# Value products of two dilated attention patterns: tokens in natural order, the permutation done by a store to and loads from DRAM

## The chip, the cores and the metric

The kernel runs on one core of a Trainium2 chip. A core has a matrix engine (TensorE, PE in the profile; its weight loads are shown apart, as PEld), a vector engine (DVE), a scalar engine (ACT), GpSimd (POOL) and SyncE (SP), which in this kernel issues every DMA. The metric is the device time of one execution in microseconds (us); less is better. Three runs of the kernel before gave 3298.71, 3296.22 and 3298.6 us, median 3298.6.

## The reference

The reference is a trunk of two layers over 1024 tokens with 1024 channels. Each layer has a mixer with four groups of heads that read the same normalised input, and a gated dense part. The change touches group D, dilated windowed attention with four heads and three patterns:

```python
D_PATTERNS = ((128, 1), (512, 4), (2048, 16))     # (window, dilation)
def to_strided(t, d):                             # tokens 0, d, 2d, ... become neighbours
    b, s, h, dh = t.shape
    return jnp.swapaxes(t.reshape(b, s // d, d, h, dh), 1, 2).reshape(b * d, s // d, h, dh)
...
o = jnp.einsum('nbhgqj,nbjhd->nbqhgd', p, vw.astype(jnp.float32)) / den
```

A pattern has its own queries, keys and values, 256 columns of the projection each. Within a residue modulo the dilation, attention is banded; the three patterns of a head meet under one softmax. What counts here is that the values of a dilated pattern are wanted ordered by (residue, index): first all tokens of residue 0, then of residue 1, and so on.

## The kernel before, in words

All products are made of three matmuls: each operand is split into a high and a low part (`hh`, `hl` for the input; `wh`, `wl` for weights), and high x high, high x low and low x high are added up in PSUM. `self.hh[k]` and `self.hl[k]`, k from 0 to 7, hold 128 channels each of the input, channels on partitions and the 1024 tokens along the free axis.

Group D runs pattern after pattern (p = 0, 1, 2): first `values(l, p)`, then for each pair of heads keys (`heads_k`), queries (`heads_q`) and scores (`scores_d`). Only when all three patterns have scores does `attend_d` multiply them with the values, through `weigh` (L628).

`values` makes values with tokens on partitions. For each of 8 token tiles it runs 8 x 3 matmuls (L587 to L589), so 192 for a pattern: the stationary operand, loaded into PE ahead of each matmul, is 128 tokens of `hh` or `hl`, and the moving operand is 256 columns of weights (288 for p = 0). The function `tokens` chooses the 128 tokens: for p = 0 neighbours, for p = 1 every fourth (residues of 4) and for p = 2 every eighth (residues of 8), so that the products come out in (residue, index) order. ACT copies each token tile from PSUM (pool `pj`, two buffers) to the tile `v` of the pattern (`put_v`, L554), beside a column of ones per head, which POOL sets once (L541).

A scheduler fixes the order of the instructions of each engine before the run; each engine works its list in order, and SP issues its DMAs in order. In layer 0 the list has work of other parts between group D's: `modulations` sums 48 pieces of a weight matrix of 256 KB each (`room<-in_w_mod`, L357 on SP; L360 and L362 on DVE; six buffers at a time; L402 to L425 fold each of three sums), and `rotary` makes tables: L329 on DVE, a sine on ACT (L331), L333 and L335 on DVE, eight transposes on PE (L340), copies on DVE (L342) and two stores `csd<-tn` on SP (L343). Layer 1 has neither within group D. Weights come from DRAM as `raw` (L116) and are split by ACT (L110) and POOL (L111). A tile of relative biases for scores comes by a DMA as well (`bias<-brep`, L601). `heads_k` and `heads_q` leave their PSUM by ACT (L507, L524) and DVE (L508, L526).

Of the kernel before, what the change touches and what calls it, by code (L numbers as in the profile page):

```python
# [48 lines left out]
DILATION = (1, 4, 8)  # L49

# [13 lines left out]
HALVES = (slice(0, 512), slice(512, 1024))  # L64

# [4 lines left out]
def _columns(name, i):  # L70
    c = np.arange(TILES_IN[name][i], TILES_IN[name][i] + 128)
    if name == "aq":
        # heads i and 2 + i: the key heads 0 and 1
        c = np.concatenate([np.arange(64 * i, 64 * i + 64), np.arange(64 * i + 128, 64 * i + 192)])
    return c
# [17 lines left out]
class Trunk:  # L93
# [14 lines left out]
    def split(self, hi, lo, src, eng=None):  # L108
        """hi + lo = src, both in the multiplier's format."""
        self.nc.scalar.activation(hi, src, AF.Copy)  # L110
        (eng or self.nc.gpsimd).tensor_sub(lo, src, hi.bitcast(F32))  # L111
# [10 lines left out]
    def gather(self, src, q, op, view=lambda x: x):  # L122
        """Reduces over the partitions; column f*32+j ends at [j, f] (rows 0..31)."""
# [16 lines left out]
    def spread(self, dst, r, f):  # L140
        """dst[p, f*32+j] = r[p//32*32+j, f]."""
        n = dst.shape[0]
        self.nc.vector.transpose(dst.rearrange("p (f i) -> p f i", i=32),
                                 r.unsqueeze(2).broadcast_to([n, f, 32]))

    def rstd(self, tiles, n, temp, adders=None):
        """Every row: rsqrt(mean over the tiles' channels of their squares + eps). The adders take turns in adding up
        the tiles."""
# [31 lines left out]
        # 3/8 of a guess at the root, a cubic step and a quadratic one  # L180
# [13 lines left out]
    def temps(self, pool=None, tag="", x=None, more=False):  # L194
        """Scratch tiles of 512 columns, from the pool or from the common ones."""
# [45 lines left out]
    def open_shared(self, name):  # L241
        """Room for the same tiles, which serves the latent attention first."""
# [18 lines left out]
    def tables(self):  # L261
        """Relative-bias rows."""
# [19 lines left out]
    def rotary(self):  # L282
        """The rotary tables."""
# [61 lines left out]
    def mod_sum(self, l, j, room=None):  # L345
        """Columns 1024*j.. of silu(c) @ w_mod[l], summed to 128 rows."""
# [19 lines left out]
    def mod_both(self, l, j, c, mr, mc):  # L366
        """As mod_sum for half c of the columns; the tensor engine takes the last of them, to one partition."""
# [18 lines left out]
    def mod_end(self, part):  # L386
        """mod[l] columns 1024*j .. with channels on partitions, b_mod added."""
# [8 lines left out]
    def mod_fold(self, part, t):  # L396
        """As mod_end, on the vector engine."""
# [15 lines left out]
    def mod_put(self, l, j, at, n, m):  # L413
# [3 lines left out]
        # scales and gates meet the norms' weights  # L417
# [15 lines left out]
    def modulated(self, src, l, g, j, hs, temp, adders=None, rs=None, ks=range(KT)):  # L433
        """hh, hl = split of rms_norm(src) * gain + shift, some of the tokens."""
# [14 lines left out]
    def residual(self, y, l, g, hs, xsrc, dst, temp, adders=None, rs=None):  # L449
        """y <- x + gain * rms_norm(y), also to dst."""  # L450
# [14 lines left out]
    def mm3(self, ps, wh, wl, xh, xl, first, last):  # L465
        """ps += w.T @ x with both split."""
# [5 lines left out]
    def product(self, ps, wh, wl, hs):  # L472
        """ps = w.T @ h for some of the tokens, the weights' low parts last."""
# [9 lines left out]
    def project(self, l, name, i, halves=(0, 1)):  # L483
        """A 128-channel tile of h @ w_in, yields (half, psum)."""
# [8 lines left out]
    def perm(self, ap, r):  # L493
        """View of natural token order on an axis that is kept as (residue, index)."""
# [18 lines left out]
    def heads_q(self, l, name, i, r=1):  # L513
        """High parts of each head on both halves of the partitions; low parts beside zeros."""
# [14 lines left out]
    def tokens(self, ap, tt, r):  # L529
        """128 columns of a [128, 1024] tile: token tile tt of the (residue, index) order."""  # L530
        if r == 1:
            return ap[:, 128 * tt:128 * tt + 128]
        n = 8 // r
        return ap.rearrange("p (l r) -> p r l", r=r)[:, tt // n, 128 * (tt % n):128 * (tt % n) + 128]

    def new_v(self, tag, heads, pool=None):
        """Room for the values, a column of ones after each head's, 32 columns after the last. Returns views of a
        token tile and head with 32 columns after the values, and of some token tiles' values."""
        v = (pool or self.vp).tile([128, 2112], F32, name="v", tag=tag)
        n = 520 * heads  # L540
        self.nc.gpsimd.memset(v[:, 0:n].rearrange("p (t c) -> p t c", c=65)[:, :, 64:65], 1.0)  # L541
# [8 lines left out]

        return taken, put
# [4 lines left out]
    def values_a(self, l):  # L556
        """Values of two heads, by way of channels on partitions, by halves of the tokens."""
# [12 lines left out]
    def values(self, l, p):  # L570
        """Values with tokens on partitions, for four heads; the first pattern's come with the latents' rotary key."""
# [3 lines left out]
        v, dst = self.new_v(f"v{p}", 4, (self.vp, self.sp, self.ub)[p])  # L575
# [5 lines left out]
        for tt in range(8):  # L581
            ps = self.pj.tile([128, 512], F32, name="pv", tag="pj")
            for k in range(KT):
                wh, wl = ws[k // n]
                cs = slice(w * (k % n), w * (k % n) + w)
                xh, xl = self.tokens(self.hh[k][:], tt, r), self.tokens(self.hl[k][:], tt, r)
# [3 lines left out]
            self.put_v(dst, tt, ps[:, :256])  # L590
            if extra:
                nc.scalar.activation(self.kr[:, tt, :], ps[:, 256:w], AF.Copy)
        return v

    def bias_tile(self, row, kind):
        """bias[k, f] = row[f - k + 127]."""
# [8 lines left out]
    def behind(self):  # L605
        """Keeps the scores of the units in order on the tensor engine."""
        return self.tc.issue_after(self.last.ins) if self.last is not None else ExitStack()

    def scores(self, ps, ks, kt, q, q0, q1, first=True):
        """The high rows of ks meet both parts of q, the low rows the high part."""  # L610
# [7 lines left out]
    def weigh(self, o, v, h, pieces, s, n, scale=1.0, seen=None):  # L618
        """o += [V.T P; 1 P; ..] with P = exp(scale * s). A piece is (token tile, a column of the last part
        of s it needs, columns of s, columns of o)."""  # L620
# [11 lines left out]
    def denominators(self, o, q, nat=lambda x: x, out=lambda x: x):  # L632
        """The row sums (rows 64..95 of o), column f*32+j at [j, f]."""
# [4 lines left out]
    def normalise(self, dst, src, q, b, den, nat=lambda x: x, out=lambda x: x):  # L638
        """dst = src (64 rows) over the denominators."""
# [66 lines left out]
    def group_a(self, l):  # L706
# [3 lines left out]
        if l:  # L710
            # what the first half of the tokens can do ahead of the second
# [16 lines left out]
    def scores_d(self, p, h, ks, q):  # L728
        """Scores of one dilated pattern; s has its queries in (residue, index) order. The third pattern
        (distances of 16) is taken by residues of 8, with the odd distances masked."""  # L730
# [50 lines left out]
    def attend_d(self, h, units, vs):  # L781
        """The three patterns of a head under one softmax; o has its even queries first."""
# [24 lines left out]
    def modulations(self):  # L807
        """The next modulations, a step each, where the scores will be."""
# [62 lines left out]
    def latents(self, l):  # L871
        """Normalised latents, split."""
# [19 lines left out]
    def key_rope(self):  # L892
        """Rotated keys, twice, tokens on partitions."""
# [13 lines left out]
    def key_rows(self, kt):  # L907
        """The rotated keys on rows 64..95 and again on 96..127, split."""
# [25 lines left out]
    def group_c(self, l, lat, kr, v, wuk, wuq):  # L934
# [22 lines left out]
        def queries(h):  # L957
            qh = self.qp.tile([128, S], F32R, name="qh", tag="qh")
            ql = self.qlc[h % 2]
            for half in range(2):  # L960
# [5 lines left out]
                # the halves of a rotated pair's sum meet the key in rows of their own  # L966
# [21 lines left out]
        # the last head needs no way through memory  # L988
# [38 lines left out]
    def mixer(self, l):  # L1027
        tc, nc = self.tc, self.nc
        with ExitStack() as e:
# [4 lines left out]
            with ExitStack() as e2:  # L1034
                self.qlp, self.bp, self.sp = p("qlp", 1, e2), p("bp", 1, e2), p("sp", 1, e2)
                self.ql = [self.qlp.tile([128, S], F32R, name=f"ql{h}") for h in range(2)]
# [29 lines left out]
    def project_out(self, l, y, between):  # L1066
        nc = self.nc
        order = ORDER_MIX
        with self.tc.tile_pool(name=f"wo{l}", bufs=1, reuse_waits="tile") as wo:
# [27 lines left out]
            # four go along as their operands come  # L1097
# [290 lines left out]
```

## Time and profile before

| what | value |
| --- | --- |
| median of three runs | 3298.6 us |
| time of the profiled execution, span | 3298.9 us |
| TensorE busy | 3066.0 us, 93% |
| VectorE, ScalarE, GpSimd busy | 62%, 32%, 29% |
| TensorE weight loads busy | 2449.6 us, 74% |
| mean granted TensorE clock | 0.977 of full |

The span runs from the first to the last instruction of the profiled execution; nothing of note lies around it, since it is within 0.3 us of the median. Matmuls and weight loads overlap in the pipeline, so the busy time of PE does not tell how fast it works: the distance between the starts of successive matmuls does.

### The profile page before, as it was taken

How to read it: one execution, taken by the hardware profiler on the slowest of the kernel's cores; microseconds unless marked ns; L12 is line 12 of the kernel's file. 1: busy time of each engine (PE TensorE's matmuls, PEld its weight loads, DVE VectorE, ACT ScalarE, POOL GpSimd, SP SyncE). 2: the span in 40 equal slices, each digit the busy share in tenths (PEclk: the TensorE clock that was granted, in tenths of full speed). 3: DMA queues.
4: the chain of work that ended last, by engine and by line, in shares of the span. 5: the costliest groups of instructions: out<-in, count | busy, mean ns of one | idle time of the engine just before them, and what ended most of it. 6: DMA issues, size and time to landing. Idle time of an engine off the chain costs nothing. (4 is left out here: it accounts for less than half of the span.)

```text
span 3298.9 us, 35152 instructions
## 1 busy us (share of the span) xinstructions
PE 3066.0 (93%) x13706; PEld 2449.6 (74%) x13706; DVE 2036.2 (62%) x2849; ACT 1064.7 (32%) x1554; POOL 953.9 (29%) x684
## 2 busy tenths in 40 slices
PE   7899988988999999999979998898889999999997
PEld 3689766776777777788746897677766788888886
DVE  6686377698666666743687524677966443434347
ACT  4221333455332222222243223435534222122222
POOL 1211132315342322223242212232244332233222
PEclk9999999999999999999989999999999999999999
DMA  5234111103322333211032100110123111111112
GB/s 202 76 99 134 36 31 33 61 17 99 122 70 90 128 117 113 90 40 63 33 124 64 47 29 28 40 46 26 33 80 118 58 51 39 39 52 58 45 39 102
DMA packets 93875, 228.62 MB, mean 69 GB/s; under 512 B 10203, under 2 KB 20699, under 8 KB 93708
## 3 DMA queue, kind: packets, MB, share of 16 engines
q1 hardware_dynamic: 93708, 226.38, 21.0%
q8 instruction: 107, 1.75, 0.2%
q14 instruction: 60, 0.49, 0.0%
HBM read 201.33 MB, written 28.41 MB: 70 GB/s over the span
## 5 line engine op out<-in xcount | busy, mean ns | idle before, releaser
L111 POOL TENSOR_TENSOR wl<-raw,wh 128x1024 fp32r<-128x1024 f32 (+2 forms) x96 | 234.2, 2448 | 835.5 <-ACT wh L110 630.6
L477 PE MATMUL pj<-hp,uh 128*128 128x512 f32 x880 | 353.2, 401 | 1.6 <-ACT hp L442 1.6
L478 PE MATMUL pj<-hp,uh 128*128 128x512 f32 x880 | 347.5, 395 | 2.9 <-POOL hp L445 2.8
L477 PE MATMUL pj<-hh,wh 128*128 128x512 f32 x800 | 327.0, 409 | 12.7 <-DVE ql L526 8.6
L478 PE MATMUL pj<-hl,wh 128*128 128x512 f32 x800 | 322.9, 404 | 3.7 <-POOL hl L445 3.5
L481 PE MATMUL pj<-hp,ul 128*128 128x512 f32 x880 | 290.1, 394 | 0.0
L111 POOL TENSOR_TENSOR ul<-raw,uh 128x1024 fp32r<-128x1024 f32 x96 | 237.3, 2474 | 162.0 <-PE pj L481 84.0
L866 DVE TENSOR_SCALAR ta<-u,par 128x1024 f32<-128x1024 f32 (+1 forms) x46 | 55.6, 1208 | 355.5 <-ACT u L1118 331.5
L477 PE MATMUL pj<-hx,uh 128*128 128x512 f32 x528 | 212.2, 402 | 11.8 <-ACT u L1118 9.2
L110 ACT ACTIVATE wh<-raw 128x1024 fp32r<-128x1024 f32 (+2 forms) x104 | 107.1, 1046 | 352.3 <-PE po L469 241.0
L481 PE MATMUL pj<-hx,ul 128*128 128x512 f32 x528 | 209.9, 397 | 0.0
L478 PE MATMUL pj<-hx,uh 128*128 128x512 f32 x528 | 207.3, 393 | 0.0
L481 PE MATMUL pj<-hh,wl 128*128 128x512 f32 x800 | 206.1, 397 | 0.0
L477 PEld LDWEIGHTS pj<-hp,uh 128*128 128x128 f32 x880 | 165.7, 188 | 45.8 <-ACT hp L442 2.2
L478 PEld LDWEIGHTS pj<-hp,uh 128*128 128x128 f32 x880 | 165.7, 188 | 44.8 <-POOL hp L445 5.5
L481 PEld LDWEIGHTS pj<-hp,ul 128*128 128x128 f32 x880 | 165.2, 188 | 39.3 <-issue 1.0
L477 PEld LDWEIGHTS pj<-hh,wh 128*128 128x128 f32 x800 | 154.1, 193 | 52.5 <-issue 14.3
L110 ACT ACTIVATE uh<-raw 128x1024 fp32r<-128x1024 f32 x100 | 105.6, 1059 | 260.0 <-DMA raw<-in_w_up_dram 137.8
L478 PEld LDWEIGHTS pj<-hl,wh 128*128 128x128 f32 x800 | 154.0, 192 | 42.6 <-POOL hl L445 5.6
L1180 DVE TENSOR_TENSOR y<-y,po 128x1024 f32<-128x1024 f32 x96 | 117.0, 1219 | 108.8 <-PE po L470 108.7
L481 PEld LDWEIGHTS pj<-hh,wl 128*128 128x128 f32 x800 | 150.8, 189 | 34.4 <-issue 0.2
L628 PE MATMUL po<-s,v 128*96 128x128 f32 (+3 forms) x672 | 131.7, 359 | 44.8 <-ACT s L625 44.7
(373 smaller groups left out, 7280.5 us busy)
## 6 DMA issues: line engine op xcount, KB each, us to landing
raw<-in_w_up_dram SPq DMA_DIRECT2D x88, 512.0 KB, 3.6
mr<-in_w_mod_dram SPq DMA_DIRECT2D x144, 256.0 KB, 3.4
raw<-in_w_in_dram SPq DMA_DIRECT2D x52, 512.0 KB, 3.5
raw<-in_w_down_dram SPq DMA_DIRECT2D x44, 512.0 KB, 3.5
room<-in_w_mod_dram SPq DMA_DIRECT2D x48, 256.0 KB, 2.9
xd<-y SPq DMA_DIRECT2D x48, 256.0 KB, 2.4
raw<-in_w_out_dram SPq DMA_DIRECT2D x16, 512.0 KB, 4.2
x<-xd SPq DMA_DIRECT2D x14, 512.0 KB, 4.4
```

Source lines behind the costliest of these rows:

```text
L110: self.nc.scalar.activation(hi, src, AF.Copy)
L111: (eng or self.nc.gpsimd).tensor_sub(lo, src, hi.bitcast(F32))
L477: nc.tensor.matmul(ps, wh[:, ks], self.hh[k][:, hs], start=k == 0, stop=False, skip_group_check=True)
L478: nc.tensor.matmul(ps, wh[:, ks], self.hl[k][:, hs], start=False, stop=False, skip_group_check=True)
L481: nc.tensor.matmul(ps, wl[:, ks], self.hh[k][:, hs], start=False, stop=k == KT - 1, skip_group_check=True)
L628: nc.tensor.matmul(o[0:96, co], v(tt, h), s[:, cs], start=co.start // 512 not in seen, stop=False, skip_group_check=True)
L866: nc.vector.tensor_scalar(o, t[:, 0:n], cw(0), None, op0=ALU.mult)
L1180: self.mark = nc.vector.tensor_add(d, d, p)
```

## The change

All three patterns take their token tiles in natural order. For p = 1 and 2, ACT copies each token tile from PSUM to a small tile `row` of 128 x 260 (four heads of 64 values and a one each; pool `vst`, two buffers; POOL sets the ones of every row), and SP stores it to a DRAM tensor `vd` in natural order. After the loop, eight loads bring the rows back to `v` in (residue, index) order, 128 rows of 1040 bytes each. Over two layers and two patterns that is 32 stores and 32 loads of 133 KB.

```diff
-    def tokens(self, ap, tt, r):
-        if r == 1:
-            return ap[:, 128 * tt:128 * tt + 128]
-        n = 8 // r
-        return ap.rearrange("p (l r) -> p r l", r=r)[:, tt // n, 128 * (tt % n):128 * (tt % n) + 128]
...
-        v, dst = self.new_v(f"v{p}", 4, (self.vp, self.sp, self.ub)[p])
+        v, dst = self.new_v(f"v{p}", 4, (self.vp, self.sp, self.ub)[p], ones=not p)
...
-                cs = slice(w * (k % n), w * (k % n) + w)
-                xh, xl = self.tokens(self.hh[k][:], tt, r), self.tokens(self.hl[k][:], tt, r)
+                cs, ts = slice(w * (k % n), w * (k % n) + w), slice(128 * tt, 128 * tt + 128)
+                xh, xl = self.hh[k][:, ts], self.hl[k][:, ts]
                 nc.tensor.matmul(ps[:, :w], xh, wh[:, cs], start=k == 0, stop=False)
                 nc.tensor.matmul(ps[:, :w], xh, wl[:, cs], start=False, stop=False)
                 nc.tensor.matmul(ps[:, :w], xl, wh[:, cs], start=False, stop=k == KT - 1)
-            self.put_v(dst, tt, ps[:, :256])
+            if p:
+                row = self.vst.tile([128, 260], F32, name="row", tag="row")
+                heads = row.rearrange("p (h c) -> p h c", c=65)
+                nc.gpsimd.memset(heads[:, :, 64:65], 1.0)
+                nc.scalar.activation(heads[:, :, 0:64], ps[:, :256].rearrange("p (h c) -> p h c", c=64), AF.Copy)
+                nc.sync.dma_start(self.vd[p - 1][128 * tt:128 * tt + 128, :], row)
+            else:
+                self.put_v(dst, tt, ps[:, :256])
...
+        if p:
+            n = 8 // r
+            rows = self.vd[p - 1].rearrange("(a p r) c -> r a p c", r=r, a=n)
+            for tt in range(8):
+                nc.sync.dma_start(v.tile[:, 260 * tt:260 * tt + 260], rows[tt // n, tt % n])
         return v
...
+                self.vst = p("vst", 2, e2)
...
+        self.vd = [dram.tile([S, 260], F32, name=f"vd{p}") for p in range(2)]
```

The change also moves instructions, in layer 0 above all. SP's list in layer 0, from the tables' first store to the weights of p = 2's values, stood like this before (a name, `<-`, its source, the shape, and how many in a row):

```order
54 L357 DMA room<-in_w_mod_dram 128x512 x3
55 L343 DMA csd<-tn 64x512
56 L357 DMA room<-in_w_mod_dram 128x512 x15
57 L116 DMA raw<-in_w_dv_dram 128x1024
```

And in the changed kernel (L592 is the store of a row, L601 its load, by the changed kernel's lines):

```order
53 L357 DMA room<-in_w_mod_dram 128x512 x7
54 L343 DMA csd<-tn 64x512
55 L357 DMA room<-in_w_mod_dram 128x512 x4
56 L343 DMA csd<-tn 64x512
57 L357 DMA room<-in_w_mod_dram 128x512 x2
58 L592 DMA vd_85<-row 128x260 x2
59 L357 DMA room<-in_w_mod_dram 128x512
60 L592 DMA vd_85<-row 128x260 x2
61 L357 DMA room<-in_w_mod_dram 128x512 x10
62 L592 DMA vd_85<-row 128x260 x2
63 L601 DMA v<-vd_85 128x260 x4
```

The first row of p = 1 is stored ahead of this place (row 50 of the list); the second and third now stand behind both stores of tables and behind pieces of the modulations, and the sixth and seventh behind ten more of them.

DVE's list in layer 0, around the end of the second modulation's sum and the keys that follow p = 1's values, stood like this before:

```order
351 L362 SCALAR_TENSOR_TENSOR room<-room,cact 128x512 x3
352 L508 TENSOR_TENSOR ks<-pj,ks 64x512
353 L362 SCALAR_TENSOR_TENSOR room<-room,cact 128x512
354 L508 TENSOR_TENSOR ks<-pj,ks 64x512
355 L362 SCALAR_TENSOR_TENSOR room<-room,cact 128x512 x2
356 L402 STREAM_TRANSPOSE room<-room 128x512
```

In the changed kernel, from the same place:

```order
358 L405 COPY sm<-sm 64x32
359 L406 TENSOR_TENSOR sm<-sm 64x32
360 L407 COPY sm<-sm 32x32
361 L408 TENSOR_TENSOR sm<-sm 32x32
362 L410 COPY sm<-sm 32x8 x4
363 L416 TENSOR_TENSOR mod<-sm,par 128x8
364 L423 SCALAR_TENSOR_TENSOR gm<-mod,par 128x8
365 L508 TENSOR_TENSOR ks<-pj,ks 64x512 x2
```

The first L508 used to stand among the last pieces of the second sum; now the whole sum and its fold (L402 to L423) stand ahead of it. In layer 1 the order of PE is unchanged.

## Rows read from the trace of the kernel before

**Rows 1.** The page: busy time by engine, and the chain that ended last.

```profile
PE 3066.0 (93%) x13706; PEld 2449.6 (74%) x13706; DVE 2036.2 (62%) x2849; ACT 1064.7 (32%) x1554; POOL 953.9 (29%) x684
...
PE 32%; DVE 10%; ACT 2%; issue 1%; POOL 1%; DMA 0%; POOLq 0%; SPq 0%; DVEq 0%; ACTq 0%
```

**Rows 2.** Windows over p=1's values in layer 0, then p=2's in layer 1.

```profile
core 0: us, PE busy (x) PEld busy (x) DVE busy (x) ACT busy (x) POOL busy (x), PEclk, DMA share, GB/s
222.00:269.00 47.00, 47.00 (x203) 45.99 (x202) 34.45 (x77) 6.01 (x13) 4.83 (x3) 0.98 0.61 196
...
1952.00:1999.00 47.00, 47.00 (x212) 46.77 (x212) 10.29 (x11) 4.95 (x10) 2.38 (x1) 1.00 0.03 9
```

**Rows 3.** Timeline of ACT, layer 0: evictions of value tiles; start, length, [wait before].

```profile
227.92 0.38 ACT L554 ACTIVATE v<-pv 128x256 f32<-128x256 f32 x1 [5.83 <-PE pv L589]
...
245.61 0.38 ACT L554 ACTIVATE v<-pv 128x256 f32<-128x256 f32 x1 [5.90 <-PE pv L589]
...
268.04 0.39 ACT L554 ACTIVATE v<-pv 128x256 f32<-128x256 f32 x1 [1.69 <-PE pv L589]
...
327.16 0.39 ACT L554 ACTIVATE v<-pv 128x256 f32<-128x256 f32 x1 [5.40 <-PE pv L589]
...
344.53 0.39 ACT L554 ACTIVATE v<-pv 128x256 f32<-128x256 f32 x1 [1.77 <-PE pv L589]
```

**Rows 4.** Timeline of PE: matmuls whose stationary operand is 128 neighbouring columns.

```profile
184.65 0.30 PE L587 MATMUL pv<-wh,hh 128*128 128x288 f32 x1
...
185.32 0.29 PE L589 MATMUL pv<-wh,hl 128*128 128x288 f32 x1
...
634.03 0.28 PE L929 MATMUL pj<-ukl,ckvh 128*128 128x256 f32 x1
...
634.50 0.28 PE L930 MATMUL pj<-ukh,ckvl 128*128 128x256 f32 x1
```

**Rows 5.** Timeline of PE's weight loads: p=0, p=1 and p=2.

```profile
184.65 0.19 PEld L588 LDWEIGHTS pv<-wl,hh 128*128 128x128 f32 x1
...
246.91 0.33 PEld L588 LDWEIGHTS pv<-wl,hh 128*128 128x128 f32 x1
...
330.69 0.34 PEld L588 LDWEIGHTS pv<-s,hh 128*128 128x128 f32 x1
```

**Rows 6.** DMA issues: KB each, median us from issue to landing.

```profile
csd<-tn SPq DMA_DIRECT2D x2, 128.0 KB, 2.4
...
bias<-brep SPq DMA_DIRECT2D x8, 128.0 KB, 2.9
```

**Rows 7.** Groups by line on POOL: count, busy us, mean ns.

```profile
L542 POOL MEMSET v<- 128x32 f32 x10 | 1.2, 121 | 0.0
```

**Rows 8.** Timeline of DVE, ACT and PE in layer 0: tables, sums, first keys.

```profile
236.82 0.22 DVE L329 TENSOR_SCALAR tb<-tb 128x128 f32<-128x128 f32 x1
...
239.41 0.30 ACT L331 ACTIVATE ta<-tb 128x128 f32<-128x128 f32 x1
...
244.30 1.04 PE L340 MATMUL pm<-ident,ta 128*64 128x128 f32 x8
...
255.01 0.17 DVE L425 TENSOR_TENSOR gm<-mod,par 128x8 f32<-128x8 f32 x1
...
256.61 4.69 DVE L362 SCALAR_TENSOR_TENSOR room<-room,cact 128x512 f32<-128x512 f32 x6
...
274.22 0.68 DVE L508 TENSOR_TENSOR ks<-pj,ks 64x512 fp32r<-64x512 f32 x1 [9.38 <-ACT ks L507]
```

**Rows 9.** Timeline of SP in layer 0: the stores of the tables.

```profile
245.65 0.45 SPq L343 DMA_DIRECT2D csd<-tn  x1
...
249.86 0.45 SPq L343 DMA_DIRECT2D csd<-tn  x1
```

**Rows 10.** Timeline of PE: first products with the values, layers 0 and 1.

```profile
430.21 0.63 PE L628 MATMUL po<-s,v 128*96 128x96 f32 x2 [4.15 <-ACT s L625]
...
2051.05 0.47 PE L628 MATMUL po<-s,v 128*96 128x96 f32 x1 [4.63 <-ACT s L625]
```

More of the change, by code (lines that the diff above doesn't have):

```diff
@@ L527, in heads_q, with new_v @@
         return list(zip(qh, self.ql))
-    def tokens(self, ap, tt, r):
-        if r == 1:
-            return ap[:, 128 * tt:128 * tt + 128]
-        n = 8 // r
-        return ap.rearrange("p (l r) -> p r l", r=r)[:, tt // n, 128 * (tt % n):128 * (tt % n) + 128]
-    def new_v(self, tag, heads, pool=None):
+    def new_v(self, tag, heads, pool=None, ones=True):
         v = (pool or self.vp).tile([128, 2112], F32, name="v", tag=tag)
         n = 520 * heads
-        self.nc.gpsimd.memset(v[:, 0:n].rearrange("p (t c) -> p t c", c=65)[:, :, 64:65], 1.0)
+        if ones:
+            self.nc.gpsimd.memset(v[:, 0:n].rearrange("p (t c) -> p t c", c=65)[:, :, 64:65], 1.0)
         self.nc.gpsimd.memset(v[:, n:n + 32], 1.0)
@@ L549, in put @@
             return v[:, 65 * heads * t0:65 * heads * t1].rearrange("p (t h c) -> p t h c", h=heads, c=65)[..., 0:64]
+        taken.tile = v
         return taken, put
```

## The prediction

> **What bounds the kernel now.** I read the page first: PE is busy for 93% of the span, and the chain that ended last lies on PE and DVE more than anywhere else [rows 1]. Busy time of a pipelined engine says little, so I went to the two stretches that the change touches. The windows show PE without a gap over the values of p = 1 in layer 0 and of p = 2 in layer 1 [rows 2], and ACT's evictions each wait for PE [rows 3]: PE paces these stretches, and every us that it needs less is a us gained, until something else is late.
>
> How fast does PE go there? Four value tiles of p = 1 take 268.04 − 245.61 = 22.43 us [rows 3], 5.61 a tile, and a tile is 24 matmuls: **0.234 us apart**. Three of p = 2 take 17.37 us, 5.79 a tile: **0.241 apart**. Elsewhere matmuls of the same 256 columns, with neighbouring columns as stationary operand, stand (634.50 − 634.03) / 4 = **0.118 apart**, and p = 0 in this same function, 288 wide, (185.32 − 184.65) / 5 = 0.134, which is 0.119 scaled to 256 columns [rows 4]. The granted clock was 0.98 and 1.00 in the strided stretches, full speed, so it is not the clock. What differs is the weight load: 0.19 us for neighbours, 0.33 at a step of four floats, 0.34 at a step of eight [rows 5]. Distance over load length is 0.70 in all three (0.134/0.19, 0.234/0.33, 0.241/0.34): the matmuls follow the loads at a fixed ratio, which is the best evidence that the loads set the pace.
>
> The Trainium skill says otherwise: "TensorE: Matmul & The Clock Gate", section LDWEIGHTS, makes a load's time depend on its count of columns alone. By that rule the natural order would give nothing. This trace does not agree: both loads have 128 columns, and 0.33 stands against 0.19.
>
> **The change part by part.**
>
> *The stationary operand becomes contiguous.* 192 matmuls a pattern and layer. p = 1: 192 × (0.234 − 0.118) = 22.2 us; p = 2: 192 × (0.241 − 0.118) = 23.6. Two layers: **91.6 us is the most that it can give**. A tile then takes 24 × 0.118 = 2.83 us in place of 5.6 to 5.8.
>
> *A row's way to DRAM.* A tile is evicted by the same ACT copy (0.38 us [rows 3]), now to `row`, of which there are two. A row is free again after eviction 0.38, SP's issue 0.45 [rows 9], landing and the ones of POOL (0.12, the nearest row being a memset of similar size [rows 7]). The trace has no store of 133 KB of this shape; the nearest are 2.4 us for 128 KB stored and 2.9 for 128 KB loaded [rows 6], and I take 2.4. The round trip is about 3.4 us against two tiles' 5.7. Without other work on SP, PE does not wait; at 2.9 it is still 3.9. It costs nothing as long as SP is free, and PE holds once the landing exceeds 4.7.
>
> *Loads of the values.* 32 loads and 32 stores at 0.45 are 29 us of SP's time, over 80 us and more per layer, with SP otherwise waiting. The values are first read at 430.21 and at 2051.05 [rows 10], more than 50 us after the last tile of p = 2 in either layer (344.53 in layer 0 [rows 3]; 1998 in layer 1, where the window ends [rows 2]). Hidden. Weights issued behind eight loads come up to 8 × 0.45 = 3.6 us later; they are loaded while the product before them runs, whose first half alone takes PE 5.6 us (from 268.4 to the first keys at 274.22 [rows 3, 8]), so I count nothing; if that cover is gone in all four places it costs up to 14 us.
>
> *Layer 1.* DMA is at 0.03 and DVE at 10.29 of 47 us [rows 2], and the order of PE is unchanged. I take off 2 us for p = 1 and 0.4 for p = 2, where the scores between the value tiles come sooner than their bias, whose load takes 2.9 [rows 6]: 20.2 + 23.2 = **43.4 us**. Bounds: 45.8 with no wait at all, 34 if each of four biases holds PE for its whole load (4 × 2.9 = 11.6).
>
> *Layer 0, p = 1.* Here the stores stand behind other work. PE starts these values at 227.92 − 5.6 = 222.3 [rows 3]; four tiles end at 233.6. Next in PE's list come the eight transposes of the tables, which need L335, which needs ACT's L331, which needs DVE's L329, over at 237.04 [rows 8]. In the run before, L331 started only at 239.41 [rows 8], after the eviction of the third tile (two tiles behind 227.92, so at 239.1); it can now start at 237.1, and with its 0.30 and two DVE copies L335 ends near 238.2. PE waits from 233.6 to 238.3: **4.7 us of the gain are lost**. The fifth tile ends at 242.2. The sixth needs the PSUM of the fourth, which leaves to the second row's buffer, whose store is in SP's list behind both `csd` stores and behind pieces of the modulations. Those wait for DVE. The transposes move up by 6 us from 244.30 [rows 8], and the table copies by nearly as much: the second `csd` was issued at 249.86 [rows 9] and now comes near 244.5; two pieces later the row is stored near 247, lands at 249.5, and PE goes on at about 249.9: **another 7.7 us lost**. Three tiles more, and p = 1 ends at 258.4 in place of 268.0: 22.2 − 4.7 − 7.7 = 9.8 gained. If the pieces pass by 242 this second wait is nothing; if they take as long as before (store at 250.5) it is 11.
>
> Then the keys: the first L508 came at 274.22 and waited only for its PSUM copy [rows 8]. It would be ready at about 264.5, but now stands behind the whole second sum: 14 pieces at 0.74 to 0.78 (six take 4.69 [rows 8]), two starts and a fold of some 4.5 us, 16 to 17 us from the end of the first fold, which was at 255.18 and I put at 251. That is 267.6, 3 us late, and the other half of the key product (5.6 us of PE) covers it. Nothing taken off; 7 us if the first fold stays at 255.
>
> *Layer 0, p = 2.* The last third of the modulations lies among these tiles, and DVE, which also puts the scores, is fuller. I take off 2.4 of 23.6 for it; the ends are 0 and 12. Layer 0 in all: 9.8 + 21.2 = **31 us**.
>
> **Sum.** 31 + 43.4 = 74.4. Against the profiled execution's span of 3298.9 that is 3224.5; the median of the runs is 0.3 lower, so I forecast **3224 us**.
>
> **The rivals.**
>
> *The full gain.* If SP's pieces do not hold the rows, and the lost time in layer 0 is made up behind p = 1 because DVE catches up, all 91.6 us come: **3207 us**. For it: DVE is busy 34.45 of 47 us in p = 1, so it has slack [rows 2]. Against it: the modulations' pieces come in turn, six buffers at a time, at 196 GB/s, and the order puts keys behind them.
>
> *Layer 0 gives nothing.* The chain of pieces, folds and stores sets layer 0's time, and PE only waits more: 43.4 us, **3255 us**. For it: DVE's share there, and the list of SP. Against it: 48 pieces at 0.78 and three folds of 4.5 are 51 us of DVE, in a stretch of 346 − 222 = 124.
>
> *The load is not the cause.* The distance of 0.234 stays because something else in these patterns sets it. Then nothing comes from PE, and the SP waits are too short to show under 5.6 us tiles: 0 to +8 us, **3299 to 3307**. The fixed ratio of distance to load speaks against it. The skill's rule on columns is its ground.
>
> *Slower: the row's round trip.* If a store of 128 rows of 1040 bytes lands late, two row buffers make PE's pace: (0.95 + landing) / 2 a tile. It equals the old 5.7 at a landing of 10.4 us, and from there the kernel is slower; at 12 us it is 6.5 a tile, 32 × 0.8 = 25 us: **3324 us**. For it: DMA is 0.61 busy in layer 0. Against it: 2.4 and 2.9 us [rows 6].
>
> **How the numbers follow.** Forecast (3216 to 3236): 0.58. Full gain, 3206 to 3216: 0.12. Layer 0 gives nothing or nearly, 3236 to 3258: 0.20. Load not the cause: 0.05, half of it within 0.2%. Round trip: 0.05. A measurement of this kernel can tell about 0.2%, 6.6 us, from no change. Faster by more than that: 0.58 + 0.12 + 0.20 = 0.90, same 0.03, slower 0.07. The range from **3206 to 3257** holds the first three cases.
>
> **What would show it.** Right: loads of L584 to L586 in the changed kernel at 0.19 us for all patterns, matmuls 0.118 apart, and evictions 2.8 apart in layer 1; in layer 0's p = 1, two gaps of PE of 4 to 8 us, the first ended by DVE or ACT at the transposes, the second by the eviction that waits for the row; landings of `vd` and `v` between 2 and 4 us; no wait of L628 for `v`. Wrong: loads that stay at 0.33; gaps of PE at each second tile in layer 1, which would be the round trip; a first L508 that holds PE for more than 5 us; or weights of the next projection that arrive after PE wants them.

## The result, and the profile after

The changed kernel took 3238.9 us (median of four runs, 3236.8 to 3243.4) against 3298.65 before: ratio 0.9817, interval 0.9803 to 0.9831, so **59.8 us less**. A second measurement beside other kernels gave 0.9821 (0.9806 to 0.9836). The forecast was 3224, 74.4 less, in a range of 3206 to 3257: the range held, the gain was overestimated by 14.6 us. The profiled execution was the fastest of the four (span 3234.9 us, 64.0 below the profile of before).

The page after, busy time by engine, answers to [rows 1]:

```profile
PE 2985.9 (92%) x13706; PEld 2365.9 (73%) x13706; DVE 2029.7 (63%) x2849; ACT 1063.9 (33%) x1554; POOL 956.7 (30%) x712
```

The view of the tile `pv` after has a group of its weight loads, all three patterns together (count: ns min/median/max, first and last start us, shape); it answers to [rows 5]:

```profile
L584 PEld LDWEIGHTS pv<-wh,hh x208: 186/188/338, 175.3 to 1933.0; 128*128 128x128 f32 x104
```

The median load was 330 ns before and is 188 now. The timeline of PE in layer 1, p = 2, shows what follows from it.

```profile
1926.69 0.28 PE L584 MATMUL pv<-wh,hh 128*128 128x256 f32 x1
1926.81 0.28 PE L585 MATMUL pv<-wl,hh 128*128 128x256 f32 x1
1926.93 0.28 PE L586 MATMUL pv<-wh,hl 128*128 128x256 f32 x1
```

The matmuls stand 0.118 us apart, as forecast. So the gain is where it was said to be. What is missing shows in layer 0. The timeline of ACT after, over p = 1's and p = 2's evictions there, answers to [rows 3]:

```profile
227.49 0.39 ACT L591 ACTIVATE row<-pv 128x256 f32<-128x256 f32 x1 [4.17 <-PE pv L586]
230.33 0.39 ACT L591 ACTIVATE row<-pv 128x256 f32<-128x256 f32 x1 [2.46 <-PE pv L586]
...
236.06 0.37 ACT L591 ACTIVATE row<-pv 128x256 f32<-128x256 f32 x1
...
251.17 0.66 ACT L591 ACTIVATE row<-pv 128x256 f32<-128x256 f32 x2 [12.56 <-DMA vd<-row]
256.99 0.39 ACT L591 ACTIVATE row<-pv 128x256 f32<-128x256 f32 x1 [5.16 <-PE pv L586]
259.59 0.39 ACT L591 ACTIVATE row<-pv 128x256 f32<-128x256 f32 x1 [2.21 <-PE pv L586]
264.94 0.38 ACT L591 ACTIVATE row<-pv 128x256 f32<-128x256 f32 x1 [3.00 <-DMA vd<-row]
...
300.62 0.39 ACT L591 ACTIVATE row<-pv 128x256 f32<-128x256 f32 x1 [3.90 <-PE pv L586]
...
323.87 0.38 ACT L591 ACTIVATE row<-pv 128x256 f32<-128x256 f32 x1 [0.50 <-PE pv L586]
```

The fourth eviction waits 12.56 us for a store of a row. SP's timeline tells why:

```profile
241.27 0.45 SPq L343 DMA_DIRECT2D csd<-tn  x1
241.78 2.85 SPq L357 DMA_DIRECT2D room<-in_w_mod_dram  x4
244.89 0.45 SPq L343 DMA_DIRECT2D csd<-tn  x1
245.54 1.58 SPq L357 DMA_DIRECT2D room<-in_w_mod_dram  x2
247.22 0.99 SPq L592 DMA_DIRECT2D vd<-row  x2
```

The second row, evicted at 230.33, is stored at 247.22, behind the tables and the pieces. In PE's timeline over the same stretch, these rows before the end of p = 2 show a wait:

```profile
239.39 1.91 PE L340 MATMUL pm<-ident,ta 128*64 128x128 f32 x8 [3.54 <-DVE ta L333]
251.61 0.58 PE L584 MATMUL pv<-wh,hh 128*128 128x256 f32 x1 [6.95 <-ACT row L591]
274.58 0.48 PE L477 MATMUL pj<-hh,wh 128*128 128x512 f32 x1 [1.19 <-DVE ks L508]
281.51 0.47 PE L477 MATMUL pj<-hh,wh 128*128 128x512 f32 x1 [1.09 <-DVE ks L508]
288.23 0.36 PE L625 MATMUL psc<-ql,ks 128*128 128x192 f32 x1 [0.80 <-DVE ql L526]
290.49 0.55 PE L584 MATMUL pv<-wh,hh 128*128 128x256 f32 x1 [1.64 <-DVE ql L526]
294.94 0.58 PE L624 MATMUL psc<-qh,ks 128*128 128x256 f32 x1 [3.26 <-DVE s L747]
302.65 0.39 PE L624 MATMUL psc<-qh,ks 128*128 128x256 f32 x1 [0.23 <-DVE s L747]
```

The two forecast gaps are there, and then a run of waits for DVE between p = 1 and p = 2. The windows show DVE nearly full there (39.94 of 45 us) and PE's clock down to 0.84 and 0.88 of full (2.4 GHz):

```profile
core 0: us, PE busy (x) PEld busy (x) DVE busy (x) ACT busy (x) POOL busy (x), PEclk, DMA share, GB/s
222.00:252.00 30.00, 19.51 (x131) 17.44 (x130) 27.94 (x66) 4.92 (x12) 4.01 (x5) 0.84 0.71 224
252.00:297.00 45.00, 37.01 (x185) 31.39 (x185) 39.94 (x57) 12.40 (x19) 11.53 (x9) 0.88 0.74 238
```

To compare kernels by stage I count from the start of the first eviction of p = 0's values in layer 0, because the stretch ahead of it differs from run to run (180.4 us before, 181.7 after, up to 188.1 in the runs below). Each number is the difference of two starts on ACT; "attention C" is the first copy of the latent attention's scores out of PSUM in layer 0, which comes after group D. The column "no row buffers" is from the second of its two profiles.

| us from first eviction of p = 0 | before | after | no row buffers | stores by ACT | sums behind queries | sums moved to C | sums cut | p = 1 alone | p = 2 alone |
| --- | --- | --- | --- | --- | --- | --- | --- | --- | --- |
| layer 0, p = 1, last eviction | 87.6 | 83.3 | 71.9 | 71.8 | 73.6 | 71.8 | 72.3 | 84.6 | 87.7 |
| layer 0, p = 2, first eviction | 121.0 | 119.0 | 110.0 | 112.0 | 102.3 | 100.5 | 101.0 | 120.1 | 120.9 |
| layer 0, p = 2, last eviction | 164.1 | 142.2 | 134.0 | 135.1 | 125.3 | 122.2 | 122.7 | 163.7 | 144.7 |
| layer 0, attention C | 469.9 | 446.7 | 439.0 | 439.9 | 439.0 | 436.9 | 428.7 | 469.7 | 449.0 |
| layer 1, p = 0, last | 1672.3 | 1648.7 | 1642.6 | 1641.1 | 1640.1 | 1656.3 | 1631.5 | 1670.2 | 1648.3 |
| layer 1, p = 1, last | 1743.7 | 1699.2 | 1693.0 | 1691.4 | 1690.4 | 1706.7 | 1681.9 | 1720.7 | 1719.7 |
| layer 1, p = 2, last | 1817.6 | 1753.5 | 1747.4 | 1746.2 | 1745.0 | 1761.2 | 1736.4 | 1796.1 | 1773.5 |

So the change gained 164.1 − 142.2 = **21.9 us in layer 0** (31 forecast), (1817.6 − 1672.3) − (1753.5 − 1648.7) = **40.5 in layer 1** (43.4 forecast), and some 2.8 elsewhere, in this pair of profiles.

### The profile page after: what moved, and what is told of

It is laid out like the page before. It is cut to its first block, busy times and chain, and to the rows that moved or that the text cites. A ratio compares the mean times of both kernels' runs of the same rounds, so it can differ in the third digit from the quotient of the medians.

```text
span 3234.9 us, 35358 instructions
## 1 busy us (share of the span) xinstructions
PE 2985.9 (92%) x13706; PEld 2365.9 (73%) x13706; DVE 2029.7 (63%) x2849; ACT 1063.9 (33%) x1554; POOL 956.7 (30%) x712
## 5 line engine op out<-in xcount | busy, mean ns | idle before, releaser
L111 POOL TENSOR_TENSOR wl<-raw,wh 128x1024 fp32r<-128x1024 f32 (+2 forms) x96 | 234.5, 2451 | 663.7 <-ACT wh L110 472.4
L477 PE MATMUL pj<-hp,uh 128*128 128x512 f32 x880 | 352.6, 401 | 1.6 <-ACT hp L442 1.6
L478 PE MATMUL pj<-hp,uh 128*128 128x512 f32 x880 | 347.1, 394 | 2.9 <-POOL hp L445 2.8
L477 PE MATMUL pj<-hh,wh 128*128 128x512 f32 x800 | 327.9, 410 | 14.2 <-DVE ql L526 8.5
L478 PE MATMUL pj<-hl,wh 128*128 128x512 f32 x800 | 323.2, 404 | 3.7 <-POOL hl L445 3.2
L111 POOL TENSOR_TENSOR ul<-raw,uh 128x1024 fp32r<-128x1024 f32 x96 | 238.5, 2486 | 162.5 <-PE pj L481 84.7
L477 PE MATMUL pj<-hx,uh 128*128 128x512 f32 x528 | 212.5, 403 | 12.6 <-ACT u L1128 10.0
L478 PE MATMUL pj<-hx,uh 128*128 128x512 f32 x528 | 207.7, 393 | 0.0
L477 PEld LDWEIGHTS pj<-hp,uh 128*128 128x128 f32 x880 | 165.6, 188 | 45.6 <-ACT hp L442 2.2
L478 PEld LDWEIGHTS pj<-hp,uh 128*128 128x128 f32 x880 | 165.5, 188 | 44.9 <-POOL hp L445 5.5
L477 PEld LDWEIGHTS pj<-hh,wh 128*128 128x128 f32 x800 | 154.4, 193 | 54.0 <-issue 17.0
L478 PEld LDWEIGHTS pj<-hl,wh 128*128 128x128 f32 x800 | 154.1, 193 | 41.8 <-POOL hl L445 5.4
L1128 ACT ACTIVATE u<-pj 128x512 f32<-128x512 f32 x176 | 103.7, 593 | 209.1 <-PE pj L481 209.1
```

Source lines behind the costliest of these rows:

```text
L477: nc.tensor.matmul(ps, wh[:, ks], self.hh[k][:, hs], start=k == 0, stop=False, skip_group_check=True)
L478: nc.tensor.matmul(ps, wh[:, ks], self.hl[k][:, hs], start=False, stop=False, skip_group_check=True)
L1128: nc.scalar.activation(u[:, 1 + 512 * half:513 + 512 * half], ps, AF.Copy)
```

## The experiments

Two theories of the missing part were set against each other. A: the modulations' sums on DVE set the end of the keys and queries in layer 0, and waits for rows matter little. B: the rows' stores behind SP's pieces are what layer 0 lost. Each kernel was measured beside the kernel before on the same chip; differences are of those medians. The kernel before took 3302.6 to 3304.6 us there, so a time in an expectation that counts from its 3298.65 is to be read as a difference.

### No row buffers, and the permutation left out

```diff
-            if p:
-                row = self.vst.tile([128, 260], F32, name="row", tag="row")
...
-                nc.sync.dma_start(self.vd[p - 1][128 * tt:128 * tt + 128, :], row)
-            else:
-                self.put_v(dst, tt, ps[:, :256])
+            self.put_v(dst, tt, ps[:, :256])
+            if p:
+                nc.sync.dma_start(self.vd[p - 1][128 * tt:128 * tt + 128, :], v.tile[:, 260 * tt:260 * tt + 260])
```

> The row buffers are taken out: a token tile is copied to its natural place in the tile of the values itself, stored to DRAM from there, and the loads come back into the same tile; nothing waits for a buffer to be stored. Theory A (in layer 0 the modulations' sums on DVE and their DMAs set the end of the keys and queries between p = 1 and p = 2, so PE's wait for rows is not what the miss is made of): the gap of 6.95 us before the sixth tile goes, the last L526 ahead of p = 2 stays within 3 us of 296.9, and the time stays within 4 us of the changed kernel's, 3235 to 3243. Theory B (the rows' stores behind SP's pieces are what layer 0 lost): some 9 us less than the changed kernel, 3227 to 3232.

Measured: 3236.7 against 3304.6, ratio 0.9797 (0.9782 to 0.9812), 68.0 us less. A second measurement beside other kernels:

> The kernel without row buffers once more, beside the two: 64 to 71 us below the kernel before, so 5 to 10 below the changed kernel.

It gave 68.7 less, 0.9795 (0.9776 to 0.9814). The list of DVE also changes: the first keys stand among the second sum's pieces again, as before the change. In the first of the two profiles PE's timeline over layer 0's p = 1 has a wait at the transposes only; behind p = 1 it waits for DVE, at the keys and at the scores,

```profile
244.06 1.92 PE L340 MATMUL pm<-ident,ta 128*64 128x128 f32 x8 [3.56 <-DVE ta L333]
...
277.29 0.47 PE L477 MATMUL pj<-hh,wh 128*128 128x512 f32 x1 [2.49 <-DVE ks L508]
...
290.41 0.58 PE L619 MATMUL psc<-qh,ks 128*128 128x256 f32 x1 [4.92 <-DVE s L742]
```

and ACT's last four evictions of p = 1 come at PE's pace:

```profile
249.60 0.39 ACT L549 ACTIVATE v<-pv 128x256 f32<-128x256 f32 x1 [2.98 <-PE pv L586]
252.44 0.39 ACT L549 ACTIVATE v<-pv 128x256 f32<-128x256 f32 x1 [2.45 <-PE pv L586]
255.28 0.39 ACT L549 ACTIVATE v<-pv 128x256 f32<-128x256 f32 x1 [2.46 <-PE pv L586]
258.12 0.39 ACT L549 ACTIVATE v<-pv 128x256 f32<-128x256 f32 x1 [0.30 <-PE pv L586]
```

p = 1 ends 11.4 us sooner than in the changed kernel, and 8.2 of them are left at the end of p = 2. Theory B had some 9, theory A at most 4: the rows did cost, and A alone falls. But the last L526 comes at 108.9 us from the first eviction in place of 115.2, so 5 of the 11.4 us are already lost again there: DVE behind p = 1 is a bound too, as theory A has it.

The permutation left out:

```diff
-            if p:
+            if False:
                 row = self.vst.tile([128, 260], F32, name="row", tag="row")
...
-        if p:
+        if False:
             n = 8 // r
```

> Natural order, the tiles copied straight to the values' tile, no store and no load: the permutation is left out, so the values stand in natural order, and the order of DVE's list around the first keys is that of the kernel before. Both theories: layer 1 gains what the changed kernel does, some 40 us, or up to 4 us more if the rows held PE there. A: the time within 5 us of the changed kernel, 3234 to 3241. B: 3225 to 3230. If the loads and stores themselves delay other transfers, both come lower by that, and a time under 3222 would say that the trip costs more than either theory has.

Measured: 3229.8, ratio 0.9777 (0.9761 to 0.9794), 74.9 us less. Group D of layer 0 and of layer 1 go as without row buffers (p = 2 ends at 132.5, attention C at 439.1; layer 1's two patterns take 104.5 us against 104.8). Stores and loads themselves cost group D next to nothing. The 6 to 7 us that this kernel is faster by lie outside group D, after layer 0's attention, where it has no instruction that the other lacks; I don't know their cause.

### The stores issued by ACT, with both row buffers kept

```diff
-                nc.sync.dma_start(self.vd[p - 1][128 * tt:128 * tt + 128, :], row)
+                nc.scalar.dma_start(self.vd[p - 1][128 * tt:128 * tt + 128, :], row)
```

> The changed kernel with its two row buffers, but ACT issues the stores right behind each eviction, so they no longer stand behind the tables' stores and the sums' pieces in SP's list; the list of DVE comes out with the first keys among the second sum's pieces again. If SP's list held the rows, the gap of 6.95 us before the sixth tile of p = 1 goes, p = 1 ends 71 to 75 us after the first eviction of p = 0 (83.3 in the changed kernel, 71.9 without row buffers) and the time is 64 to 72 us below the kernel before. If two buffers are too few by themselves, p = 1 ends after 79 and the time is that of the changed kernel, 56 to 63 below.

Measured: 3233.4 against 3302.6, ratio 0.9789 (0.9774 to 0.9804), 69.2 us less. ACT's timeline in layer 0:

```profile
248.04 0.39 ACT L591 ACTIVATE row<-pv 128x256 f32<-128x256 f32 x1 [2.78 <-PE pv L586]
248.50 0.33 ACTq L592 DMA_DIRECT2D vd<-row  x1
250.88 0.39 ACT L591 ACTIVATE row<-pv 128x256 f32<-128x256 f32 x1 [2.46 <-PE pv L586]
251.34 0.33 ACTq L592 DMA_DIRECT2D vd<-row  x1
253.72 0.39 ACT L591 ACTIVATE row<-pv 128x256 f32<-128x256 f32 x1 [2.46 <-PE pv L586]
```

Each row is on its way 0.46 us after its eviction starts, and the evictions stand 2.84 us apart on the same two buffers. The count of buffers was not the trouble; the place of the stores in SP's list was. Within the intervals this is as fast as no row buffers at all, and both beat the changed kernel by 8 to 9 us. The intervals of the two sides touch, but the profiles agree: attention C comes at 438.8 to 439.9 us in the three without the hold, at 446.7 and 447.2 in the two of the changed kernel.

### The trip alone, and each pattern alone

```diff
-                cs, ts = slice(w * (k % n), w * (k % n) + w), slice(128 * tt, 128 * tt + 128)
-                xh, xl = self.hh[k][:, ts], self.hl[k][:, ts]
+                cs, rr = slice(w * (k % n), w * (k % n) + w), r
+                xh, xl = self.tokens(self.hh[k][:], tt, rr), self.tokens(self.hl[k][:], tt, rr)
...
-                nc.sync.dma_start(v.tile[:, 260 * tt:260 * tt + 260], rows[tt // n, tt % n])
+                nc.sync.dma_start(v.tile[:, 260 * tt:260 * tt + 260], self.vd[p - 1][128 * tt:128 * tt + 128, :])
```

> The other half alone: the stationary operand is strided as in the kernel before, and the tiles still go through rows, store and load (in (residue, index) order, so the loads permute nothing). Weight loads at 0.33 and 0.34 us and matmuls 0.234 and 0.241 apart; both theories: no gain, 3297 to 3310, at most two gaps of PE in layer 0. If the gain came from anything in the rows' way and not from the load, this would stand near 3239.

Measured: 3314.1 against 3304.6, ratio 1.003 (1.0018 to 1.0042): slower by some 9 us. The weight loads' median is 330 ns again, and p = 1 of layer 0 ends 5.8 us later than before, for one eviction waits 15.65 us for `vd<-row`. A line of the view of the tile `pv`, and one of ACT's timeline:

```profile
L590 PEld LDWEIGHTS pv<-wh,hh x208: 187/330/341, 181.5 to 2004.7; 128*128 128x128 f32 x104
```

```profile
263.46 0.66 ACT L597 ACTIVATE row<-pv 128x256 f32<-128x256 f32 x2 [15.65 <-DMA vd<-row]
```

So nothing of the gain comes from the rows' way, and the forecast that SP's waits would be "too short to show" under slow tiles (0 to 8 us) was wrong.

For each pattern alone the other keeps `tokens` and the copy straight to its tile (q is 1 or 2):

```diff
-                xh, xl = self.hh[k][:, ts], self.hl[k][:, ts]
+                xh, xl = self.tokens(self.hh[k][:], tt, rr), self.tokens(self.hl[k][:], tt, rr)
...
-            if p:
+            if p == q:
```

> Only p = 1 takes natural order and the way through DRAM. If the stages add up, this and the kernel with p = 2 alone (41 us) make the changed kernel's 60: 18 to 23 us below the kernel before, nearly all of it from layer 1 (20.9), with the first eviction of p = 2 in layer 0 at 118 to 121 us after p = 0's first, as before. If the two changes get in each other's way, it is over 26.

> Only p = 2 takes natural order and the way through DRAM; p = 1 stays strided and is copied straight to its tile. From the stages of the changed kernel's profile, p = 2 gained 20 us in layer 0 and 19.6 in layer 1, while p = 1 gained nearly nothing in layer 0 (its rows held PE and the sums took the rest) and 20.9 in layer 1. So 38 to 44 us less than the kernel before, and the first p = 2 eviction of layer 0 within 3 us of the kernel before's. If the rows of p = 1 had cost p = 2 something, it would be more: over 45.

(`rr` is 1 for p = q.) Measured: p = 1 alone 18.1 us less (0.9941, 0.9925 to 0.9957), p = 2 alone 40.8 less (0.9881, 0.9864 to 0.9899). 18.1 + 40.8 = 58.9, the changed kernel's 60 within the intervals: they add up. In the table p = 1 alone has nothing left of its gain at the end of layer 0's p = 2 (163.7 against 164.1).

### The sums out of the way

In the next kernels `modulations` changes; they build on the one without row buffers unless said otherwise.

```diff
-        for j in (2, 4, 3):
+        for j in (2,):
...
+            if l == 0 and h in (0, 2):
+                part = self.mod_sum(0, (4, 3)[h // 2])
+            if l == 0 and h in (1, 3):
+                self.mod_fold(part, self.mr.tile([128, 512], F32, name="mr", tag="mr"))
```

> As the kernel without row buffers, and the second and third sum of the modulations are taken out of group D of layer 0 and made during the latent attention. A: the keys and queries between p = 1 and p = 2 are no longer held by DVE, and layer 0's group D ends 9 to 15 us sooner: 3222 to 3232, if the latent attention hides the sums. B: as the kernel without row buffers, within 4 us.

Measured: 3250.2, ratio 0.9838 (0.9823 to 0.9852), 54.4 less: 13.6 slower than without row buffers, where theory A had expected a gain. The table shows both halves of it: p = 2's values end 11.8 us sooner (122.2 against 134.0), as theory A wants it, and at attention C 2 are left; by layer 1 it is behind. DVE had no room there. In the 71 us ahead of attention C it is busy 56.69 us in place of 41.13 of 65 in the kernel without row buffers, and PE has 57.75 of 71 in place of 60.49 of 65.

```diff
+            with self.tc.issue_after(self.query.ins) if j in (4, 3) else ExitStack():
                 part = self.mod_sum(0, j, room)
```

(`self.query` is the last L526; the fill ahead of p = 1's values moves behind its keys and queries.)

> As the kernel without row buffers, and in layer 0 the second and third sum of the modulations start on DVE only after the last L526 of the queries between p = 1 and p = 2; they lie beside p = 2's values and stay in group D. If the sums on DVE are what held the keys and queries, group D of layer 0 ends 8 to 12 us sooner than without row buffers, and nothing later gives it back as the latent attention did: 72 to 82 us less than the kernel before. If those 12 us came back only because the sums had left group D altogether, nothing is gained: 62 to 70 less. If p = 1's scores are now held by the third sum, under 62.

Measured: 3236.4 against 3304.5, ratio 0.9794 (0.9780 to 0.9809), 68.2 less, the same as without row buffers and short of the 72 to 82 expected. p = 2 ends 8.7 us sooner, and attention C comes at 439.0 as if nothing had been done. ACT shows where it went: the next keys wait for DVE, which is still at the third sum.

```profile
326.35 1.05 ACT L507 ACTIVATE ks<-pj 64x512 fp32r<-64x512 f32 x1 [7.71 <-DVE ks L508]
```

> The same shift of the second and third sum in the kernel before (strided loads, no trip). PE had 3.2 us without work between p = 1 and p = 2 there (24.78 busy of 28), so the sums hardly held it: within 5 us of the kernel before. If the shift by itself were the gain, it would come out 8 to 12 us faster.

Measured: 0.9989 (0.9980 to 0.9998), 4.6 us less, inside what was expected: with strided loads it was mostly PE, not DVE, that paced this part (p = 2 ends 3.7 us sooner, 160.4 against 164.1).

Last, the sums without seven of eight pieces, nowhere paid for:

```diff
-            for k in range(KT):
+            for k in range(1 if room else KT):
```

> The kernel without row buffers, and each of the three sums of the modulations in group D of layer 0 takes one of its eight pieces for each half only (7 of 8 are left out, in DMA and on DVE; the folds stay). If the sums are what kept layer 0 from its share, nothing has to be paid for them elsewhere now: counted from the first eviction of p = 0, p = 2's values end at 118 to 124 (134.2 without row buffers, 142.2 in the changed kernel, 164.1 before; the full gain would be 118.3), and the latent attention's first eviction comes 10 to 14 us sooner than without row buffers, at 425 to 429; the time is 76 to 86 us below the kernel before. If something else holds group D, it stays at 436 to 440, and the time within 5 us of the kernel without row buffers.

Measured: 3226.7 against 3303.3, ratio 0.9767 (0.9751 to 0.9783), 76.6 less. p = 2 ends at 122.7, and attention C comes at 428.7, 10.3 us sooner: what the sums took stays gained when they need not be made. This run leaves out the pieces' transfers together with DVE's work on them, so it shows what the sums cost as a whole, not how much of it is DVE's part. The remaining 4 us to the full gain (164.1 less 45.8, so 118.3) hold the one wait of PE left in group D's values, at the transposes:

```profile
241.84 1.44 PE L340 MATMUL pm<-ident,ta 128*64 128x128 f32 x8 [3.89 <-DVE ta L333]
```

The changed kernel once more served as the control beside the second set:

> The changed kernel once more, beside these: 56 to 64 us less than the kernel before. Milestones of layer 0 and 1 as in its first profile within 2 us, counted from the first eviction of p = 0's values.

Measured: 60.1 less (0.9821), and its milestones agree with the first profile's: 83.6, 142.6 and 447.2 in layer 0, 1753.5 at the end of layer 1's p = 2.

## Why the prediction was right, and where it was off

**The load sets the pace**: that the step of the stationary operand does is shown. Without it loads took 0.19 us and matmuls stood 0.118 apart, as forecast, the same with the trip left out; with it kept there was no gain at all. That it works through the load's length is argued from the rows, 0.33 and 0.34 us where matmuls stand 0.234 and 0.241 apart. The forecast's "best evidence", a fixed ratio of 0.70, was chance: its 0.134 belongs to products of 288 columns, and the products of 256 that it compares stand at 0.118 / 0.188 = 0.63. With neighbouring columns and the same loads of 0.19 us, the distance goes with the columns that move, 0.118 for 256, 0.134 for 288, 0.234 for 512 (L477 and L478, from 1831.79 in the trace of after), so there the load is not the pace. The forecast's sum doesn't hang on the ratio, since 0.118 was read from rows of its own. The rival that the load is not the cause falls, and so does the rule of the Trainium skill ("TensorE: Matmul & The Clock Gate", section LDWEIGHTS) as a full account: loads of 128 columns took 330 or 188 ns by their step alone.

**The round trip does not bind**: right. Stores landed in 1.8 us (2.4 taken), loads in 4.2 (a little over the 2 to 4 foreseen). With SP's list out of the way, two buffers were enough.

**Layer 1**: 40.5 of 43.4. p = 1 gave 20.9 (20.2 forecast), p = 2 19.6 (23.2), and the same without the trip (104.5 us for both patterns), so rows and loads are not the reason. PE's windows of after have 2.3 us without work between p = 1's last and p = 2's first eviction and 1.2 behind that, 3.5 in all against 1.24 before; most of it is waits for DVE (L526 1.18 and 0.70, L508 0.63, L752 0.43), none directly for a bias. The keys, queries and scores on DVE had been covered by longer value tiles. This is 2.3 of the 3.6; the rest I could not place.

**Layer 0, p = 1**: the two holds were right in place, cause and size (3.54 for 4.7, 6.95 for 7.7), and the stores' place in SP's list is confirmed by the run with ACT's queue. Left out was what a wait costs afterwards: from the transposes to the end of p = 1 (239.39 to 262.09) PE took 15.75 us besides the second wait, where the forecast has 12.4, at a granted clock of 0.50 behind that wait. So two misses in part cancelled, waits 1.9 us shorter and work 3.4 us longer than forecast. PE ended p = 1 at 262.1 (first L477 behind it), 80.4 us after the first eviction, 78.0 by the forecast.

**The keys behind p = 1: the step that failed.** It said that the fold would end at 267.6 and that "nothing" was to be taken off. PE's first key product started 7.0 us sooner than before (80.4 against 87.4), and p = 2's first eviction only 2.0 sooner, of which 3.0 are that tile's own: **7.9 us were lost** there, the largest single miss. Some 4.8 of them are longer waits of PE (8.0 us in the five rows above from 274.58 to 294.94, against 3.2 in the same stretch before); the rest goes with a lower clock behind these waits (granted 0.62 from 287.2 to 300.6, against 0.84 in the same part before). The first fold ended at 250.8 (L425), where the forecast put it (251); from there the second sum and its fold took 21.6 us in place of 16 to 17, to 272.4, as DVE's timeline shows:

```profile
252.22 0.49 DVE L360 TENSOR_SCALAR room<-room,cact 128x512 f32<-128x512 f32 x1 [1.42 <-DMA room<-in_w_mod_dram]
...
261.17 4.34 DVE L362 SCALAR_TENSOR_TENSOR room<-room,cact 128x512 f32<-128x512 f32 x3 [1.65 <-DMA room<-in_w_mod_dram]
...
272.21 0.17 DVE L423 SCALAR_TENSOR_TENSOR gm<-mod,par 128x8 f32<-128x8 f32 x1
272.40 0.69 DVE L508 TENSOR_TENSOR ks<-pj,ks 64x512 fp32r<-64x512 f32 x1
```

Two sizes were off. DVE waited 4.4 us for pieces (2.7 ahead of L360, 1.7 ahead of L362 between 252 and 297; 3.3 of it ahead of the fold), and L362 took 970 ns on average in place of 740 to 780: three of them took 4.34 us while POOL ran a 2.95 us L111 beside them, and again at 281.40 beside the L111 of 281.64. POOL's timeline:

```profile
262.01 2.95 POOL L111 TENSOR_TENSOR wl<-raw,wh 128x1024 fp32r<-128x1024 f32 x1 [7.37 <-ACT wh L110]
```

The 14 traces of this case have this pattern throughout. Of 518 L362 around layer 0's group D, the 468 with no such work of POOL beside them took 0.70 to 0.76 us. Just 29 took longer, 2.1 to 3.0 us; each of them lay beside an L111 and ended 0.5 to 0.6 us behind its end. An L362 that was running when the L111 began kept its 0.75 us. No run took the L111 away, but no row speaks against it as the cause. Up to the fold it cost 2.1 us, which with the 3.3 of waiting makes up the fold's delay. And one thing was looked at too narrowly: the forecast followed the first L508, but the queries, the third sum and the scores behind it stood in the same full list of DVE. The rival "layer 0 gives nothing" had named this bound; it holds for the part from p = 1 to p = 2, not for p = 2's own tiles, which gave 22.8 us (19.9 between its first and last eviction and 3.0 in the first tile; 21.2 forecast).

So of the 74.4 forecast, 9.1 failed in layer 0 (9.8 − 7.0 = 2.8 in p = 1, 7.9 in the keys, 1.6 better in p = 2) and 2.9 in layer 1, which leaves 62.4; 2.8 came elsewhere, 1.2 was lost ahead of p = 0's first eviction, and the two profiles differ by 64.0. The medians differ by 4.2 less than this pair of profiles.

## What to carry to other kernels

When a change makes one engine twice as fast in a stretch, count the other engines' work of the stretch as a whole against its new length: here sums that PE's slow tiles had covered became the bound, and moving them only moved the loss, twice. A store that frees a buffer belongs in a queue where nothing waits ahead of it: the same two row buffers cost p = 1 11 us behind SP's list and nothing on ACT's. And before a strided stationary operand is taken for harmless, the distance of its matmuls should be compared with the same product's at unit step: here it was double.

## What the hardware showed beside

With strided loads the clock hardly mattered here. After the gaps PE ran at a granted 0.50, 1.2 GHz, in both kernels (window 264.0 to 268.8 of the trip alone, 252.0 to 255.5 after); the trip's strided matmuls then stood 0.235 us apart, against 0.234 at full clock, while the contiguous ones stood 0.213 apart in place of 0.118. The loads go with that: strided ones took 0.33 us at either clock, contiguous ones 0.33 at 1.2 GHz (after, 252.20 to 255.40) and 0.19 at 2.4. The timeline of PE after, and of the trip alone:

```profile
252.41 0.41 PE L584 MATMUL pv<-wh,hh 128*128 128x256 f32 x1
...
255.40 0.41 PE L586 MATMUL pv<-s,hl 128*128 128x256 f32 x1
...
255.79 0.28 PE L585 MATMUL pv<-s,hh 128*128 128x256 f32 x1
...
256.03 0.28 PE L584 MATMUL pv<-s,hh 128*128 128x256 f32 x1
```

```profile
264.53 0.44 PE L592 MATMUL pv<-wh,hl 128*128 128x256 f32 x1
...
266.65 0.44 PE L592 MATMUL pv<-wh,hl 128*128 128x256 f32 x1
```

(14 matmuls from 252.41 to 255.40, 9 from 264.53 to 266.65.) A wait therefore cost the fast stretch more than the slow one: behind the gap of 6.95, 19 matmuls took 4.18 us (251.61 to 255.79), some 1.9 more than at 0.118. The loads from DRAM differ too, by groups of DMA issues (KB, median us to landing), first after, then the trip alone:

```profile
v<-vd SPq DMA_DIRECT2D x32, 130.0 KB, 4.2
```

```profile
v<-vd SPq DMA_DIRECT2D x32, 130.0 KB, 2.1
```

It looks like the price of taking rows of 1040 bytes every fourth or eighth, but the two differ in another way as well: after issued its loads in bursts, for the most part 0.4 to 0.5 us apart within a burst, the trip alone mostly 5 to 8 us apart. A load of every fourth row that led a burst (after, issued at 1871.69) landed in 2.07 us, and two loads of the trip alone that stood 0.47 us apart (276.48 and 276.95) in 2.51 and 2.79. So a cost of the step is not shown; the rows speak for the bursts.
